# Down projection of a gated MLP in seven block products: all operand sums on VectorE, another order of the products, splits and sums on pairs of tiles

## The chip, the cores and the metric

The kernel runs on one core of a Trainium2 chip. The time is the device time of one launch in microseconds (us), the median of several executions. The core's engines work side by side, each through its own queue in order: PE (TensorE, matrix products into PSUM), DVE (VectorE, elementwise), ACT (ScalarE, elementwise with a function), POOL (GpSimd, elementwise here) and SP (SyncE, which in this kernel only issues DMA transfers). They are tied together by semaphores that a planner has placed.

## The reference, cut to what matters

One layer: three token mixers on 1024 tokens and 256 context tokens, merged into a residual stream, then a gated MLP with a depthwise convolution of three taps, then a final RMS norm. What the change touches is the last matrix product of the MLP and what follows it:

```python
def conv_ffn(h, w_up, w_dw, b_dw, w_down):
    a, g = jnp.split(dwconv(h @ w_up, w_dw, b_dw), 2, axis=-1)
    return (a * jax.nn.silu(g)) @ w_down          # (1024, 2816) @ (2816, 1024)
...
    x = x_mix + m_lat[:, :, 5] * conv_ffn(h, ...)
return rms_norm(x, norm_final)
```

All in fp32. The kernel computes an fp32 product by splitting each operand into a rounded high part and the rest (`hi`, `lo`), and adding three passes on PE: hi·hi, hi·lo, lo·hi.

## The kernel before

**The down projection** (from line 961 on, the last stage) is a 2 x 2 block product in Winograd's form, with seven block products instead of eight. The 2816 features are cut into two halves of 11 tiles of 128 (`KD = 11`), the 1024 tokens into two halves of 512 (`LH`), the 1024 output channels into two halves of four tiles. The activations lie in DRAM (`act_d`), as blocks B11 (first feature half, first token half), B12 (first, second), B21, B22; the weights as W11, W12, W21, W22 (`w_dn`). Each product `q` (0 to 6) multiplies one activation block or sum of blocks by one weight block or sum of blocks: 11 feature tiles x 4 output tiles x 3 passes = 132 matmuls of 128 x 128 by 512 columns. In `q` = 6 the loops are turned round (output tile outside), and its last output tile is done in 384 and 128 columns (`LAST`).

| q | activation operand | weight operand | PSUM set | added to `xt` afterwards (token half, first channel tile) |
|---|---|---|---|---|
| 0 | B11 | W11 | 0, new | (0, 0) |
| 1 | t = B22 - B12, on POOL | s = W11 - W21, on POOL | 1, new | (1, 4) |
| 2 | t + B11, on DVE | s = W22 - s, on POOL | 0, goes on | (1, 4), (0, 4), (1, 0) |
| 3 | B21 - t, on POOL | W22 | 1, goes on | (0, 4) |
| 4 | B12 - B11, on POOL | W11 + s, on POOL | 0, new | (1, 4) |
| 5 | B21 | W12; s = W12 - s on POOL for q = 6 | 1, new | (0, 0) |
| 6 | B22 | s | 0, goes on | (1, 0) |

`act(q, k)` (line 990) makes the activation operand of one feature tile: it loads what it needs (`load_b1`, and `stream`, which uses two buffers for B12 and three for the others), forms the sum, and calls `split`: a cast on ACT to `hi` (line 738) and a subtraction on DVE to `lo` (line 739), into one of 12 buffers `ac`. `weights(q, k0, nk)` (line 1032) does the same for the weights of two feature tiles (a pair; the eleventh is alone): raw weights through three buffers `wr`, a resident copy `dw` of 11 tiles that holds the running sum, and `w_split` (lines 1026 and 1027) into three buffers each of `wh` and `wl`. `dn` (lines 1067 to 1069) issues the three passes. After each product `add` (line 1075) adds the PSUM tiles, scaled by a channel's factor, to the residual `xt`, 36 additions in all (one of them in two pieces), in groups of four by `after` (line 1082). When a tile of `xt` is complete, `done` squares it on ACT and sums the squares, on POOL for the first of them (line 735). `final` scales by the norm and stores; two of its eight tiles go over POOL (line 1096).

**What sets the order.** A planner orders each engine's queue by priority, in the order of the program, with work moved ahead by `tc.high_priority(offset=...)`: sums and loads of a later unit come ahead of the earlier unit's matmuls by `APRIO + SPRIO` or `WPRIO + SPRIO` places. At run time each queue is strictly in order; an instruction that waits holds up all behind it, on SP too.

```python
  1004                        G.tensor_tensor(out=src, in0=b, in1=a, op=ALU.subtract)
  1051                        G.tensor_tensor(out=s, in0=s, in1=r, op=ALU.subtract)
  1055                        G.tensor_tensor(out=s, in0=r, in1=s, op=ALU.subtract)
  1082        after = (((0, 0, 0),), ((1, 4, 0),), ((1, 4, 0), (0, 4, 0), (1, 0, 0)), ((0, 4, 1),), ((1, 4, 1),), ((0, 0, 1),))
  1108            new = q in (0, 1, 4, 5)
```

(`G` is POOL, `V` is DVE, `A` is ACT, `T` is PE.)

Of the kernel before, what the change touches and what calls it, by code (L numbers as in the profile page):

```python
# [85 lines left out]
def build(tc, ins, out):  # L86
    nc = tc.nc
    V, A, G, T, SP = nc.vector, nc.scalar, nc.gpsimd, nc.tensor, nc.sync
    with ExitStack() as top:
# [635 lines left out]
        def sumsq(pool, parts, src, i, name, n, NPOOL):  # L725

            first = i in (0, NPOOL, KT - 1)
            sq = pool.tile([P, n], F32, tag="ss" if first and i < KT - 1 else "sq", name=f"ss{name}{i}",
                           bufs=3 if first and i < KT - 1 else 2)
            A.activation(sq, src, AF.Square)  # L730
            if first:
                parts.append(sq)
            else:
                e, q = (G, parts[0]) if i < NPOOL else (V, parts[1])
                e.tensor_tensor(out=q, in0=q, in1=sq, op=ALU.add)
# [228 lines left out]
        NRING = 12  # L964
        B11, B12, B21, B22 = range(4)
        b1 = [(pa if k < 8 else p2).tile([P, LH], F32, tag=f"b1_{k}", name=f"b1_{k}") for k in range(KD)]
        tt = {}
        dw = p2.tile([P, KD, 512], F32, tag="dw", name="dw")

        def load_b1(k):  # L970
            SP.dma_start(b1[k], act_d[k][:, t1])

        def stream(b, k, q):
            if b == B12:
                t = pc.tile([P, LH], F32, tag="sn", name=f"b{b}_{q}_{k}", bufs=2)
            else:
                t = p2.tile([P, LH], F32, tag="st", name=f"b{b}_{q}_{k}", bufs=3)
            SP.dma_start(t, act_d[b // 2 * KD + k][:, t2 if b % 2 else t1])
            return t

        def t_tile(k):
            if k not in tt:
                if k == KD - 1:
                    tt[k] = p2.tile([P, LH], F32, tag="tt", name="tt")
                else:
                    t = pc.tile([P, 2, LH], F32, tag="c", name=f"tt{k}", bufs=NC)
                    tt[k], tt[k + 1] = t[:, 0], t[:, 1]
            return tt[k]

        def act(q, k):  # L990
            j = (q * KD + k) % NRING
            t = pa.tile([P, 2, LH], F32R, tag=f"ac{j}", name=f"ac{q}_{k}")
            h = t[:, 0], t[:, 1]
            with tc.high_priority(offset=APRIO):
                with tc.high_priority(offset=SPRIO):
                    if q == 0:
                        load_b1(k)
                        src = b1[k]
                    elif q == 1:
                        if k < 2:  # L1000
                            load_b1(k)
                        a, b = stream(B12, k, q), stream(B22, k, q)
                        src = t_tile(k)
                        G.tensor_tensor(out=src, in0=b, in1=a, op=ALU.subtract)
                    elif q == 2:
                        src = tt[k]
                        V.tensor_tensor(out=src, in0=src, in1=b1[k], op=ALU.add)
                    elif q == 3:
                        b = stream(B21, k, q)
                        src = tt[k]  # L1010
                        G.tensor_tensor(out=src, in0=b, in1=src, op=ALU.subtract)
                    elif q == 4:
                        b = stream(B12, k, q)
                        src = b1[k]
                        G.tensor_tensor(out=src, in0=b, in1=src, op=ALU.subtract)
                    else:
                        src = stream((B21, B22)[q - 5], k, q)
                split(h, src)
            return h

        def w_split(src, nk, ncol):

            cnt[0] += 1
            hi, lo = (wp.tile([P, 1024], F32R, tag=t, name=f"{t}{cnt[0]}", bufs=n)[:, :nk * ncol]
                      .rearrange("p (k n) -> p k n", k=nk) for t, n in (("wh", WH), ("wl", WL)))
            A.copy(hi, src)
            V.tensor_tensor(out=lo, in0=src, in1=hi.bitcast(F32), op=ALU.subtract)  # L1027
            return hi, lo

        W11, W12, W21, W22 = (ins["w_dn"][j] for j in range(4))  # L1030

        def weights(q, k0, nk):

            def raw(src):
                cnt[0] += 1
                t = wp.tile([P, 1024], F32, tag="wr", name=f"wr{cnt[0]}", bufs=WR)[:, :nk * 512]
                t = t.rearrange("p (k n) -> p k n", k=nk)
                SP.dma_start(t, src[k0:k0 + nk].rearrange("f p t -> p f t"))
                return t

            s = dw[:, k0:k0 + nk]
            with tc.high_priority(offset=wprio[0]):
                with tc.high_priority(offset=SPRIO if q else 0):
                    if q == 0 and k0 >= 4:
                        SP.dma_start(s, W11[k0:k0 + nk].rearrange("f p t -> p f t"))
                        src = s
                    elif q == 1:
                        if k0 < 4:
                            SP.dma_start(s, W11[k0:k0 + nk].rearrange("f p t -> p f t"))
                        r = raw(W21)  # L1050
                        G.tensor_tensor(out=s, in0=s, in1=r, op=ALU.subtract)
                        src = s
                    elif q == 2:
                        r = raw(W22)
                        G.tensor_tensor(out=s, in0=r, in1=s, op=ALU.subtract)
                        src = s
                    else:
                        src = raw((W11, None, None, W22, W11, W12)[q])
                        if q == 4:
                            G.tensor_tensor(out=src, in0=src, in1=s, op=ALU.add)  # L1060
# [18 lines left out]
        def done(tb, i, n):  # L1079
            sumsq(p2, sss[tb], xts[tb][:, i], n, f"f{tb}", LH, NPOOL)  # L1080

        after = (((0, 0, 0),), ((1, 4, 0),), ((1, 4, 0), (0, 4, 0), (1, 0, 0)), ((0, 4, 1),), ((1, 4, 1),), ((0, 0, 1),))
# [18 lines left out]
        first = [(a0[0][:, f], a0[1][:, f]) for f in range(2)]  # L1101
        wprio[0] = WPRIO_D
        sets = [None, None]
        xload = [(tb, i) for tb, i0 in ((0, 0), (1, 4), (0, 4), (1, 0)) for i in range(i0, i0 + 4)]
        count = [0, 0]
        for q in range(6):
            st = q % 2
            new = q in (0, 1, 4, 5)
# [7 lines left out]
            for k0 in range(0, KD, 2):  # L1116
                nk = min(2, KD - k0)
                w = weights(q, k0, nk)
                for k in range(k0, k0 + nk):
                    h = first.pop(0) if first else act(q, k)  # L1120
                    for j in range(4):
                        dn(zs[j], [p[:, k - k0] for p in w], slice(j * P, (j + 1) * P), h, new and k == 0, k == KD - 1, **on)
                if pend and k0 == 2:
                    act_store()
                if k0 >= 4:
                    for _ in range(2 if q == 2 else 1):
                        if xload:
                            tb, i = xload.pop(0)
                            SP.dma_start(xts[tb][:, i], xm_d[tb, i])
                if q == 0 and k0 == 4:  # L1130
                    wprio[0] = WPRIO
            for tb, i0, end in after[q]:
                for j in range(4):
                    add(tb, i0 + j, zs[j])
                    if end:
                        done(tb, i0 + j, count[tb])
                        count[tb] += 1

        q = 6
        ss = sss[1]  # L1140
        xt = xts[1]
# [3 lines left out]
        for i in range(4):  # L1145
            ws = {}
            z0 = 0
            for n in LAST if i == 3 else (LH,):
                z = sets[0][i][:, z0:z0 + n]
                for f0 in range(0, KD, 8):  # L1150
# [4 lines left out]
                    for k in range(f0, f0 + nk):  # L1155
                        if k not in hs:
                            hs[k] = act(q, k)
                        dn(z, [p[:, k - f0] for p in ws[f0]], slice(0, P), [t[:, z0:z0 + n] for t in hs[k]],
                           False, k == KD - 1, skip_group_check=True)
                    if f0 == 0 and i == 0:  # L1160
                        norm = rms_r(p2, sss[0], LH, "f0", True)
                    if f0 == 0 and i == 1:
                        final("0", norm, xts[0], 0, LH)
# [4 lines left out]
                with tc.high_priority(offset=0 if prev is None else LPRIO):  # L1168
                    add(1, i, z, z0, n)
                    if i < 3:  # L1170
                        done(1, i, 4 + i)
                        continue
                    sq = p2.tile([P, n], F32, tag="sq", name=f"ssl{z0}", bufs=2)
                    A.activation(sq, xt[:, i, z0:z0 + n], AF.Square)
                    args = ([t[:, z0:z0 + n] for t in ss] + [sq], n, f"fl{z0}", True)
                    if prev is None:
                        prev = [args, xt, LH + z0, n]
# [3 lines left out]
        final("2", r, xt, L - n, n)  # L1181
# [545 lines left out]
```

## Time and profile before

| | us |
|---|---|
| median of 3 runs (lowest, highest) | 2101.91 (2099.66, 2103.96) |
| the profiled execution | 2102.28 |
| its span, first to last instruction | 2100.5 |

A profile shows one execution of the program. Times in its views are counted from the first instruction of the span. The page's first part gives each engine's busy time:

```profile
span 2100.5 us, 30318 instructions
## 1 busy us (share of the span) xinstructions
PE 2045.0 (97%) x11501; PEld 1706.9 (81%) x11501; DVE 1460.3 (70%) x2338; ACT 1009.6 (48%) x1776; POOL 413.1 (20%) x314
```

PEld is the loading of weights, which overlaps the matmuls. A matmul's recorded length contains its pipeline, so matmuls that follow one another start closer together than they are long. The second part cuts the span in 40 slices of 52.5 us, with the busy share in tenths:

```profile
PE   8999999999999999999999999999999999997997
DVE  4846656636665788577887747569778777769983
POOL 0000000010021232100000000011332343247752
PEclk9999999999999999999999999999999999998999
```

The down projection takes the last five slices, from 1846.4 us on.

### The profile page before, as it was taken

What the parts mean: (1) busy time and instruction counts of PE and PEld (TensorE: products, weight loads), DVE (VectorE), ACT (ScalarE), POOL (GpSimd) and SP (SyncE); (2) the same over time, 40 slices, a digit from 0 to 9 for tenths busy, and PEclk for the clock granted to TensorE, in tenths of its full rate; (3) what the DMA queues carried; (4) which work ended last, traced back from release to release, by engine and by line L of the source; (5) the groups of instructions that cost most, each with busy time, mean ns of one, the idle gap of its engine ahead of it and who ended that gap; (6) DMA issues with size and microseconds to landing.
All of it is one profiled execution on the core that took longest, in us unless ns stands there. A gap on an engine that the chain in (4) does not pass through costs nothing.

```text
span 2100.5 us, 30318 instructions
## 1 busy us (share of the span) xinstructions
PE 2045.0 (97%) x11501; PEld 1706.9 (81%) x11501; DVE 1460.3 (70%) x2338; ACT 1009.6 (48%) x1776; POOL 413.1 (20%) x314
## 2 busy tenths in 40 slices
PE   8999999999999999999999999999999999997997
PEld 5888888888988888878888788888888888885886
DVE  4846656636665788577887747569778777769983
ACT  3433333311122877688888734346444444443451
POOL 0000000010021232100000000011332343247752
PEclk9999999999999999999999999999999999998999
DMA  9411111136544311211110454541222222277442
GB/s 369 135 45 34 39 51 41 46 121 215 183 137 130 96 47 54 90 37 33 36 34 23 134 193 142 192 158 54 100 81 91 72 89 81 86 252 242 141 156 81
DMA packets 101746, 227.95 MB, mean 109 GB/s; under 512 B 10976, under 2 KB 35936, under 8 KB 100576
## 3 DMA queue, kind: packets, MB, share of 16 engines
q1 hardware_dynamic: 101600, 226.02, 32.6%
q8 instruction: 90, 1.47, 0.3%
q14 instruction: 56, 0.46, 0.1%
HBM read 180.37 MB, written 45.61 MB: 108 GB/s over the span
## 4 chain that ended last, share of the span: by engine, by line
PE 65%; DVE 4%; DMA 2%; issue 2%; ACT 2%; POOL 1%; SPq 0%; DVEq 0%; POOLq 0%; ACTq 0%
PE pp L1476 4%; PE gz L190 3%; PE gz L191 3%; PE gz L192 3%; PE dn L1069 3%; PE dn L1067 3%; PE dn L1068 3%; PE up L909 2%; PE up L910 2%; PE up L911 2%; PE po L1462 2%; PE po L1463 2%; PE br L191 2%; PE br L192 2%; PE br L190 2%
## 5 line engine op out<-in xcount | busy, mean ns | idle before, releaser
L166 ACT CAST wh<-wr 128x1024 fp32r<-128x1024 f32 x91 | 95.8, 1052 | 282.9 <-PE gz L191 50.8
L167 DVE TENSOR_TENSOR wl<-wr,wh 128x1024 fp32r<-128x1024 f32 x91 | 112.5, 1237 | 105.6 <-ACT wh L166 104.5
L1481 DVE TENSOR_TENSOR pl<-pp,ph 128x512 fp32r<-128x512 f32 x236 | 159.7, 688 | 29.4 <-ACT ph L1480 23.8
L190 PE MATMUL gz<-hh,wh 128*128 128x512 f32 x384 | 156.0, 407 | 3.2 <-ACT gs L580 3.1
L191 PE MATMUL gz<-hl,wh 128*128 128x512 f32 x384 | 152.4, 397 | 0.0
L192 PE MATMUL gz<-hh,wl 128*128 128x512 f32 x384 | 152.2, 397 | 0.0
L1480 ACT CAST ph<-pp 128x512 fp32r<-128x512 f32 x236 | 135.7, 585 | 31.5 <-PE pp L1476 28.8
L1069 PE MATMUL dn<-ac,wl 128*128 128x512 f32 (+2 forms) x311 | 121.5, 391 | 13.0 <-DVE wl L1027 12.8
L1068 PE MATMUL dn<-ac,wh 128*128 128x512 f32 (+2 forms) x311 | 121.0, 389 | 2.2 <-DVE ac L739 2.2
L1067 PE MATMUL dn<-ac,wh 128*128 128x512 f32 (+2 forms) x311 | 121.1, 390 | 1.4 <-DVE xt L1075 1.4
L201 PE MATMUL tm<-wl,hh 128*128 128x256 f32 x384 | 108.9, 283 | 2.4 <-DVE wl L167 2.4
L200 PE MATMUL tm<-wh,hh 128*128 128x256 f32 x384 | 108.7, 283 | 0.0
L202 PE MATMUL tm<-wh,hl 128*128 128x256 f32 x384 | 108.6, 283 | 0.0
L1462 PE MATMUL po<-ph,VHL 128*128 128x512 f32 x236 | 106.1, 449 | 1.6 <-ACT ph L1480 1.1
L1463 PE MATMUL po<-pl,VHL 128*128 128x512 f32 x236 | 97.4, 413 | 0.1
L190 PEld LDWEIGHTS gz<-hh,wh 128*128 128x128 f32 x384 | 72.7, 189 | 16.7 <-ACT gs L580 5.3
L192 PEld LDWEIGHTS gz<-hh,wl 128*128 128x128 f32 x384 | 72.6, 189 | 15.0
L191 PEld LDWEIGHTS gz<-hl,wh 128*128 128x128 f32 x384 | 72.8, 190 | 11.3
L1069 PEld LDWEIGHTS dn<-ac,wl 128*128 128x128 f32 x311 | 59.5, 191 | 26.5 <-DVE wl L1027 14.9
L1476 PE MATMUL pp<-ident,plat 128*128 128x128 f32 x512 | 76.6, 273 | 0.0
L201 PEld LDWEIGHTS tm<-wl,hh 128*128 128x128 f32 x384 | 73.7, 192 | 3.3 <-DVE wl L167 3.0
L1476 PEld LDWEIGHTS pp<-ident,plat 128*128 128x128 f32 x512 | 62.7, 140 | 16.8 <-DVE pl L1481 1.2
(1426 smaller groups left out, 6068.9 us busy)
## 6 DMA issues: line engine op xcount, KB each, us to landing
wr<-in_w_cm SPq DMA_DIRECT2D x48, 512.0 KB, 3.8
wr<-in_w_up SPq DMA_DIRECT2D x44, 512.0 KB, 3.5
b<-act_d SPq DMA_DIRECT2D x77, 256.0 KB, 3.5
wmr<-in_w_mod SPq DMA_DIRECT2D x32, 512.0 KB, 4.5
wr<-in_w_dn SPq DMA_DIRECT2D x27, 512.0 KB, 3.8
gate_d<-gs SPq DMA_DIRECT2D x48, 256.0 KB, 2.1
sgt<-gate_d SPq DMA_DIRECT2D x24, 512.0 KB, 3.3
act_d<-u SPq DMA_DIRECT2D x22, 512.0 KB, 2.6
```

The costliest lines, as they stand in the source:

```text
L190: T.matmul(psl, wh[:, k, c], hh[:, k0 + k, cols], start=s, stop=False)
L191: T.matmul(psl, wh[:, k, c], hl[:, k0 + k, cols], start=False, stop=False)
L192: T.matmul(psl, wl[:, k, c], hh[:, k0 + k, cols], start=False, stop=e)
L201: T.matmul(psl, hh[:, k, toks], wl[:, k % 4, :], start=False, stop=False)
L1067: T.matmul(z, w[0][:, c], h[0], start=s, stop=False, **on)
L1068: T.matmul(z, w[0][:, c], h[1], start=False, stop=False, **on)
L1069: T.matmul(z, w[1][:, c], h[0], start=False, stop=e, **on)
L1462: T.matmul(po, vv, ph, start=n == 0, stop=False)
L1463: T.matmul(po, vv, pl, start=False, stop=n == len(kts) - 1)
L1476: T.transpose(pp[:, h], PT(h, n), ident)
L1480: A.copy(ph, pp)
L1481: V.tensor_tensor(out=pl, in0=pp, in1=ph.bitcast(F32), op=ALU.subtract)
```

## The change

The seven products are formed from other sums and come in another order:

| q | activation operand | weight operand | PSUM set | added to `xt` afterwards |
|---|---|---|---|---|
| 0 | B11 | W11 | 0, new | (0, 0) |
| 1 | x = B12 - B11 | s = W22 + W21 | 1, new | (1, 4) |
| 2 | x = B22 - x | s = s - W11 | 0, goes on | (1, 0) |
| 3 | B22 | W12 - s | 1, goes on | (1, 0) |
| 4 | B11 - x | s = W22 - s | 0, goes on | (1, 4) |
| 5 | B21; x = B21 - x for q = 6 | W12; W22 is loaded into `dw` for q = 6 | 1, new | (0, 0) |
| 6 | x | W22 | 0, goes on | (0, 4) |

All sums are on DVE (`less`, and one addition), as are the sums of squares in `done`. A PSUM set is added to `xt` after each product and nowhere twice: 28 additions. Loads, sums and splits of the activations work on pairs of feature tiles (`u` from 0 to 5, the last one single), with six buffers `ac` of twice the size, and the streamed blocks take the five buffers `c` (pairs, too) that the up projection used, in place of the two and three single ones. In `q` = 0 the weights all go through `wr`.

```diff
-        def sumsq(pool, parts, src, i, name, n, NPOOL):
+        def sumsq(pool, parts, src, i, name, n, NPOOL, eng=G):
...
-                e, q = (G, parts[0]) if i < NPOOL else (V, parts[1])
+                e, q = (eng, parts[0]) if i < NPOOL else (V, parts[1])
...
-        NRING = 12
+        NRING = 6
+        UN = (KD + 1) // 2
...
+        nks = [min(2, KD - 2 * u) for u in range(UN)]
+        tx = [(pa if u < 4 else p2).tile([P, nks[u], LH], F32, tag=f"tx{u}", name=f"tx{u}") for u in range(UN)]
...
+        def stream(b, q, u):
+            return fetch(pc.tile([P, 2, LH], F32, tag="c", name=f"b{b}_{q}_{u}", bufs=NC)[:, :nks[u]], b, u)
+
+        def less(out, a, b):
+            V.tensor_tensor(out=out, in0=a, in1=b, op=ALU.subtract)
+
+        def act(q, u):
+            t = pa.tile([P, 2, 2, LH], F32R, tag=f"ac{(q * UN + u) % NRING}", name=f"ac{q}_{u}")
+            h = t[:, 0, :nks[u]], t[:, 1, :nks[u]]
+            x = tx[u]
             with tc.high_priority(offset=APRIO):
+                src = x
                 with tc.high_priority(offset=SPRIO):
...
+                    if q == 0 or q == 1 and u == 0:
+                        fetch(x, B11, u)
+                    if q == 1:
+                        less(x, stream(B12, q, u), x)
                     elif q == 2:
...
+                        less(x, stream(B22, q, u), x)
                     elif q == 3:
...
+                        src = stream(B22, q, u)
                     elif q == 4:
...
+                        src = stream(B11, q, u)
+                        less(src, x, src)
+                    elif q == 5:
+                        src = stream(B21, q, u)
+                        less(x, src, x)
                 split(h, src)
             return h
...
             s = dw[:, k0:k0 + nk]
             with tc.high_priority(offset=wprio[0]):
                 with tc.high_priority(offset=SPRIO if q else 0):
...
+                    src = s
+                    if q == 0:
+                        src = raw(W11)
                     elif q == 1:
...
+                        load(s, W21)
+                        V.tensor_tensor(out=s, in0=raw(W22), in1=s, op=ALU.add)
                     elif q == 2:
...
+                        less(s, s, raw(W11))
+                    elif q == 3:
+                        src = raw(W12)
+                        less(src, src, s)
+                    elif q == 4:
+                        less(s, raw(W22), s)
                     else:
...
+                        src = raw(W12)
                 w = w_split(src, nk, 512)
                 if q == 5:
-                    G.tensor_tensor(out=s, in0=src, in1=s, op=ALU.subtract)
+                    load(s, W22)
...
-        after = (((0, 0, 0),), ((1, 4, 0),), ((1, 4, 0), (0, 4, 0), (1, 0, 0)), ((0, 4, 1),), ((1, 4, 1),), ((0, 0, 1),))
+            sumsq(p2, sss[tb], xts[tb][:, i], n, f"f{tb}", LH, NPOOL, V)
+
+        after = ((0, 0, 0), (1, 4, 0), (1, 0, 0), (1, 0, 1), (1, 4, 1), (0, 0, 1))
...
-            new = q in (0, 1, 4, 5)
+            new = q in (0, 1, 5)
...
+            for u in range(UN):
+                w = weights(q, u)
+                h = act(q, u) if q or u else a0
...
-                        final("0", norm, xts[0], 0, LH)
+                        final("0", norm, xts[1], LH, LH)
...
-                    add(1, i, z, z0, n)
+                    add(0, 4 + i, z, z0, n)
```

More of the change, by code (lines that the diff above doesn't have):

```diff
@@ L962, in build @@
         p2 = Aligned(top.enter_context(tc.tile_pool(name="p2", bufs=1, reuse_waits="tile")))
-        NRING = 12
+        NRING = 6
+        UN = (KD + 1) // 2
         B11, B12, B21, B22 = range(4)
-        b1 = [(pa if k < 8 else p2).tile([P, LH], F32, tag=f"b1_{k}", name=f"b1_{k}") for k in range(KD)]
-        tt = {}
+        W11, W12, W21, W22 = (ins["w_dn"][j] for j in range(4))
+        nks = [min(2, KD - 2 * u) for u in range(UN)]
+        tx = [(pa if u < 4 else p2).tile([P, nks[u], LH], F32, tag=f"tx{u}", name=f"tx{u}") for u in range(UN)]
@@ L968, in build @@
         dw = p2.tile([P, KD, 512], F32, tag="dw", name="dw")
[L970 to L978, printed above, removed]
-            return t
[L981 to L993, printed above, removed]
+        def fetch(t, b, u):
+            f = b // 2 * KD + 2 * u
+            SP.dma_start(t, act_d[f:f + nks[u], :, t2 if b % 2 else t1].rearrange("f p t -> p f t"))
+            return t
+        def stream(b, q, u):
+            return fetch(pc.tile([P, 2, LH], F32, tag="c", name=f"b{b}_{q}_{u}", bufs=NC)[:, :nks[u]], b, u)
@@ L994, in act @@
+        def less(out, a, b):
[4 more added lines that the diff above has]
+            x = tx[u]
             with tc.high_priority(offset=APRIO):
+                src = x
                 with tc.high_priority(offset=SPRIO):
[L996 to L1004, printed above, removed]
+                    if q == 0 or q == 1 and u == 0:
+                        fetch(x, B11, u)
+                    if q == 1:
+                        less(x, stream(B12, q, u), x)
@@ L1005, in act @@
                     elif q == 2:
-                        src = tt[k]
-                        V.tensor_tensor(out=src, in0=src, in1=b1[k], op=ALU.add)
+                        less(x, stream(B22, q, u), x)
                     elif q == 3:
-                        b = stream(B21, k, q)
-                        src = tt[k]
-                        G.tensor_tensor(out=src, in0=b, in1=src, op=ALU.subtract)
+                        src = stream(B22, q, u)
                     elif q == 4:
-                        b = stream(B12, k, q)
@@ L1014, in act @@
[L1014 to L1017, printed above, removed]
+                        src = stream(B11, q, u)
[3 more added lines that the diff above has]
+                        less(x, src, x)
                 split(h, src)
@@ L1025, in w_split, with weights, load @@
                       .rearrange("p (k n) -> p k n", k=nk) for t, n in (("wh", WH), ("wl", WL)))
-            A.copy(hi, src)
-            V.tensor_tensor(out=lo, in0=src, in1=hi.bitcast(F32), op=ALU.subtract)
+            split((hi, lo), src)
             return hi, lo
-        W11, W12, W21, W22 = (ins["w_dn"][j] for j in range(4))
-        def weights(q, k0, nk):
+        def weights(q, u):
+            k0, nk = 2 * u, nks[u]
+            def load(t, src):
+                SP.dma_start(t, src[k0:k0 + nk].rearrange("f p t -> p f t"))
+                return t
             def raw(src):
@@ L1036, in raw @@
                 t = wp.tile([P, 1024], F32, tag="wr", name=f"wr{cnt[0]}", bufs=WR)[:, :nk * 512]
-                t = t.rearrange("p (k n) -> p k n", k=nk)
-                SP.dma_start(t, src[k0:k0 + nk].rearrange("f p t -> p f t"))
-                return t
+                return load(t.rearrange("p (k n) -> p k n", k=nk), src)
             s = dw[:, k0:k0 + nk]
@@ L1043, in weights @@
                 with tc.high_priority(offset=SPRIO if q else 0):
-                    if q == 0 and k0 >= 4:
-                        SP.dma_start(s, W11[k0:k0 + nk].rearrange("f p t -> p f t"))
-                        src = s
+                    src = s
+                    if q == 0:
+                        src = raw(W11)
                     elif q == 1:
[L1048 to L1052, printed above, removed]
-                    elif q == 2:
-                        r = raw(W22)
-                        G.tensor_tensor(out=s, in0=r, in1=s, op=ALU.subtract)
-                        src = s
-                    else:
-                        src = raw((W11, None, None, W22, W11, W12)[q])
-                        if q == 4:
-                            G.tensor_tensor(out=src, in0=src, in1=s, op=ALU.add)
+                        load(s, W21)
+                        V.tensor_tensor(out=s, in0=raw(W22), in1=s, op=ALU.add)
+                    elif q == 2:
+                        less(s, s, raw(W11))
[4 more added lines that the diff above has]
+                        less(s, raw(W22), s)
+                    else:
+                        src = raw(W12)
                 w = w_split(src, nk, 512)
                 if q == 5:
-                    G.tensor_tensor(out=s, in0=src, in1=s, op=ALU.subtract)
+                    load(s, W22)
             return w
@@ L1100, in build @@
         a0 = w_unit(act_d[0:2, :, :LH].rearrange("f p t -> p f t"), 2, LH)
-        first = [(a0[0][:, f], a0[1][:, f]) for f in range(2)]
         wprio[0] = WPRIO_D
+        xload = [(tb, i) for tb, i0 in ((0, 0), (1, 4), (1, 0), (0, 4)) for i in range(i0, i0 + 4)]
+        count = [0, 0]
         sets = [None, None]
-        xload = [(tb, i) for tb, i0 in ((0, 0), (1, 4), (0, 4), (1, 0)) for i in range(i0, i0 + 4)]
-        count = [0, 0]
         for q in range(6):
             st = q % 2
-            new = q in (0, 1, 4, 5)
+            new = q in (0, 1, 5)
             if new and st:
@@ L1115, in build @@
             on = dict(skip_group_check=not new)
[L1116 to L1120, printed above, removed]
+            for u in range(UN):
+                w = weights(q, u)
+                h = act(q, u) if q or u else a0
+                for k in range(nks[u]):
                     for j in range(4):
-                        dn(zs[j], [p[:, k - k0] for p in w], slice(j * P, (j + 1) * P), h, new and k == 0, k == KD - 1, **on)
-                if pend and k0 == 2:
+                        dn(zs[j], [p[:, k] for p in w], slice(j * P, (j + 1) * P), [t[:, k] for t in h],
+                           new and k == u == 0, 2 * u + k == KD - 1, **on)
+                if pend and u == 1:
                     act_store()
[L1125 to L1130, printed above, removed]
-                    wprio[0] = WPRIO
[L1132 to L1137, printed above, removed]
+                if u >= 2 and q < 4:
+                    tb, i = xload.pop(0)
+                    SP.dma_start(xts[tb][:, i], xm_d[tb, i])
+                if q == 0 and u == 2:
+                    wprio[0] = WPRIO
+            tb, i0, end = after[q]
+            for j in range(4):
+                add(tb, i0 + j, zs[j])
+                if end:
+                    done(tb, i0 + j, count[tb])
+                    count[tb] += 1
         q = 6
-        ss = sss[1]
-        xt = xts[1]
+        ss = sss[0]
+        xt = xts[0]
         hs = {}
@@ L1156, in build @@
                         if k not in hs:
-                            hs[k] = act(q, k)
+                            h = act(q, k // 2)
+                            for c in range(nks[k // 2]):
+                                hs[k + c] = [t[:, c] for t in h]
                         dn(z, [p[:, k - f0] for p in ws[f0]], slice(0, P), [t[:, z0:z0 + n] for t in hs[k]],
@@ L1160, in build @@
                     if f0 == 0 and i == 0:
-                        norm = rms_r(p2, sss[0], LH, "f0", True)
+                        norm = rms_r(p2, sss[1], LH, "f0", True)
                     if f0 == 0 and i == 1:
-                        final("0", norm, xts[0], 0, LH)
+                        final("0", norm, xts[1], LH, LH)
                     if prev is not None and f0 == 0:
@@ L1168, in build @@
                 with tc.high_priority(offset=0 if prev is None else LPRIO):
-                    add(1, i, z, z0, n)
+                    add(0, 4 + i, z, z0, n)
                     if i < 3:
-                        done(1, i, 4 + i)
+                        done(0, 4 + i, 4 + i)
                         continue
                     sq = p2.tile([P, n], F32, tag="sq", name=f"ssl{z0}", bufs=2)
-                    A.activation(sq, xt[:, i, z0:z0 + n], AF.Square)
+                    A.activation(sq, xt[:, 4 + i, z0:z0 + n], AF.Square)
                     args = ([t[:, z0:z0 + n] for t in ss] + [sq], n, f"fl{z0}", True)
                     if prev is None:
-                        prev = [args, xt, LH + z0, n]
+                        prev = [args, xt, z0, n]
                     else:
@@ L1180, in build @@
                 z0 += n
-        final("2", r, xt, L - n, n)
+        final("2", r, xt, LH - n, n)
 def forget(nc, pool, z, F, K, bounds, n, nm, tag=None):
```

1 line of the change is left out of this document (removed).

## The prediction, made before the changed kernel ran

> **What bounds the kernel now.** The first view is the span with its clock, the second the busy time of each engine in stretches. The stretches run from one product's first matmul to the next one's, then to the end of the last product and of the span; columns are length, busy time of PE, PEld, DVE, ACT and POOL with counts, the granted clock, the DMA share and GB/s.
>
> ```profile
> core 0: 2100.5 us, clock 0.993
> ```
> ```profile
> 1846.40:1877.20 30.80, 30.65 (x133) 24.55 (x132) 19.91 (x24) 13.22 (x19) 15.13 (x7) 1.00 0.75 274
> 1877.20:1926.30 49.10, 35.58 (x133) 27.62 (x132) 47.10 (x36) 17.57 (x27) 36.34 (x19) 0.83 0.73 246
> 1926.30:1958.10 31.80, 30.23 (x133) 24.68 (x133) 31.80 (x24) 12.12 (x17) 27.37 (x16) 1.00 0.63 207
> 1958.10:1988.00 29.90, 29.90 (x134) 24.76 (x133) 26.54 (x31) 11.91 (x17) 19.66 (x9) 1.00 0.50 158
> 1988.00:2018.00 30.00, 30.00 (x134) 24.84 (x133) 25.87 (x22) 15.09 (x23) 20.54 (x9) 1.00 0.50 159
> 2018.00:2047.90 29.90, 29.90 (x133) 24.78 (x132) 25.14 (x26) 16.31 (x27) 13.99 (x8) 1.00 0.42 132
> 2047.90:2087.50 39.60, 38.16 (x212) 33.13 (x210) 15.34 (x23) 8.98 (x14) 10.40 (x7) 1.00 0.15 54
> 2087.50:2100.50 13.00, 1.69 (x10) 1.21 (x10) 5.51 (x15) 1.05 (x3) 4.19 (x6) 0.68 0.48 162
> ```
>
> Products 3, 4 and 5 take 29.9 us each with PE never idle: 132 matmuls at 0.227 us. That is PE's floor. Products 0, 1 and 2 take 30.8 + 49.1 + 31.8 = 111.7 us, against 3 x 29.9 = 89.7. **22.0 us** are lost there, 19.2 of them in product 1, where DVE is busy for 47.1 of 49.1 us. The third view, the chain of work that ended last, shows how; the fourth (timeline) gives POOL and the two longest stalls of PE.
>
> ```profile
> 1903.62 2.80 DVE tt L1007
> 1906.42 5.54 DVE ac L739 x2
> 1911.97 2.74 DVE tt L1007
> 1914.71 1.15 DVE wl L1027
> ...
> 1916.70 0.43 PE dn L1067
> ...
> 1920.96 0.43 PE dn L1068
> 1921.39 0.32 PE dn L1069
> 1921.70 0.23 PE dn L1067
> ```
> ```profile
> 1903.42 10.74 POOL L1055 TENSOR_TENSOR dw<-wr,dw 128x1024 f32<-128x1024 f32 x4 [0.95 <-DMA wr<-in_w_dn]
> 1900.79 0.80 PE L1069 MATMUL dn<-ac,wl 128*128 128x512 f32 x1 [5.07 <-DVE wl L1027]
> 1915.90 0.79 PE L1069 MATMUL dn<-ac,wl 128*128 128x512 f32 x1 [6.14 <-DVE wl L1027]
> ```
>
> While POOL forms four weight sums for product 2 (10.74 / 4 = 2.7 us each), DVE's small operations for product 1 take 2.7 to 2.8 us each, one to each POOL operation, and PE waits for `wl`. What they take without POOL is seen around 1857, where POOL has yet to start (its first sum is at 1859.0, in the `L1051` row below) and the DMA engines are full (timeline, then the stretch; the third row is from later):
>
> ```profile
> 1854.67 3.10 DVE L739 TENSOR_TENSOR ac<-b,ac 128x512 fp32r<-128x512 f32 x5
> 1857.69 2.36 DVE L1027 TENSOR_TENSOR wl<-dw,wh 128x1024 fp32r<-128x1024 f32 x2
> 2047.51 2.07 DVE L1075 SCALAR_TENSOR_TENSOR xt<-dn,mods,xt 128x512 f32<-128x512 f32 x3
> ```
> ```profile
> 1846.40:1857.00 10.60, 10.59 (x47) 8.46 (x46) 10.38 (x13) 6.95 (x11) 0.00 (x0) 1.00 1.00 366
> ```
>
> 3.10 / 5 = 0.62 us for 512 columns, 2.36 / 2 = 1.18 for 1024, 2.07 / 3 = 0.69 for an addition from PSUM. The view of one line (shortest, median, longest ns) tells who is stretched:
>
> ```profile
> L1007 DVE TENSOR_TENSOR tt<-tt,b x11: 679/694/2879, 1869.5 to 1922.8; 128x512 f32<-128x512 f32 x11
> L1075 DVE SCALAR_TENSOR_TENSOR xt<-dn,mods,xt x37: 351/739/751, 1884.1 to 2087.5; 128x512 f32<-128x512 f32 x35, 128x384 f32<-128x384 f32 x1, 128x128 f32<-128x128 f32 x1
> L1051 POOL TENSOR_TENSOR dw<-dw,wr x6: 1713/2406/5049, 1859.0 to 1897.9; 128x1024 f32<-128x1024 f32 x5, 128x512 f32<-128x512 f32 x1
> L735 POOL TENSOR_TENSOR ssf<-ssf,ssf x10: 1281/1730/2285, 1993.7 to 2068.5; 128x512 f32<-128x512 f32 x10
> ```
>
> Operations that read two SBUF tensors go up to four times their price, those that read one from PSUM never (751 ns at most), and POOL's stretch as well. So product 1 is bound by DVE and POOL getting in each other's way.
>
> **The change, part by part.** *PE* keeps its matmuls: seven products of 132, product 6 in the same pieces.
>
> *POOL's sums go to DVE.* I count product by product, with a "set" for one operation over the 11 feature tiles: five pairs and a single, 5 x 1.18 + 0.62 = 6.5 us. Products 1 and 2: activation sum, weight sum and two splits, four sets, plus four additions at 0.69: 26.0 + 2.8 = 28.8 us each. Product 3: three sets and four additions, 22.3. Product 4: four sets, four additions and three sums of squares at 0.62, 30.7. Product 5: three sets, four additions, two sums of squares, 23.5. Together 134.1 us in the 149.5 that PE needs for the five. Measured now are 47.1 + 31.8 + 26.5 + 25.9 + 25.1 = 156.4, so DVE takes over POOL's work and is still busy for 22 us less. Product 4 is 0.8 us over its 29.9; product 3, with 7.6 to spare, covers it if work runs ahead. It can: three buffers of split weights and six of split activations are three units and one whole product (a unit, a pair of tiles, is 24 matmuls, 5.4 us). If that cover were gone, product 4 would cost those 0.8.
>
> *The stall of products 0 to 2 goes:* -22.0 us, if nothing else is late. What is next is PE itself, then DVE at 28.8 of 29.9. Part of the 22.0 is clock: after the 6.14 us stall eleven matmuls start 0.43 apart instead of 0.23, 2.2 us. The Trainium skill, "TensorE: Matmul & The Clock Gate", section "What's actually happening", says that an idle window of about 3.4 us halves the clock until PE has been busy for another. By that, leftover stalls shorter than this cost their own length only, and longer ones more; the row above agrees for a stall of 6.14.
>
> *Pairs.* The first unit of product 0 that `act` makes now needs a cast and a subtraction of 1024 columns before the first matmuls, in place of 512:
>
> ```profile
> L738 ACT CAST ac<-b 128x512 fp32r<-128x512 f32 x42 | 25.0, 617 | 23.9 <-DMA b<-act_d 18.3 <-PE dn L1069 5.6
> L1026 ACT CAST wh<-dw 128x1024 fp32r<-128x1024 f32 x17 | 17.7, 1049 | 14.8 <-PE dn L1068 9.3 <-DMA dw<-in_w_dn 2.1 <-DVE wl L1027 1.8
> ```
>
> 1.05 - 0.62 + 1.18 - 0.62 = 1.0 us, once, since no lead exists there yet: +1.0 (bounds 0, as the loads may be first, and 3). Elsewhere pairs lie under PE. ACT, at most 17.6 us a product now, keeps its work.
>
> *Eight additions fewer* lie on DVE in product 2's place and are in the count. The sums of squares of product 6 (five of the ten in `L735` are of this token half) aren't what its end waits for: the row of PE's waits for DVE there is the additions, which stay, as does the tail of 13.0 us.
>
> ```profile
> PE dn L1067 <- DVE xt L1075: 1.4, 3, 0.7
> ```
>
> *Loads.* The tiles of 256 KB, by count of the code: 66 of activations for the 77 below, 88 of weights for 70. SP's queue is in order, and what held it before were POOL and DVE.
>
> ```profile
> b<-act_d SPq DMA_DIRECT2D x77, 256.0 KB, 3.5
> wr<-in_w_dn SPq DMA_DIRECT2D x27, 512.0 KB, 3.8
> ```
> ```profile
> SPq L1038 <- DVE wl L1027: 31.9, 7, 7.0
> SPq L978 <- POOL tt L1004: 25.3, 7, 8.5
> ```
>
> The second wait goes; the streams now have five pair buffers that wait for DVE. What is added is DVE's own wait: a `less` whose load is late holds the splits behind it in DVE's queue, and PE waits for those. I cost loads at nothing: DVE, PE and the lead of three units (16 us) hide landings of 4 us. If the cover goes, see the second rival.
>
> *Small DVE waits.* DVE now has slack of 1.1 us in each of products 1 and 2. In product 1 it stood waiting for ACT as follows:
>
> ```profile
> DVE ac L739 <- ACT ac L738: 6.0, 2, 4.2
> ```
>
> In product 0 DVE is idle 30.8 - 19.9 = 10.9 us, in which it can get ahead. How much of such waiting reaches PE no row shows. Bounds: 0 and 13; I take 2, near the lower end, because the lead of product 0 stands against it.
>
> Sum: 2102.28 - 22.0 + 1.0 + 2.0 = 2083.3 for the profiled execution. That execution is 0.4 above the median of the three runs, so the same number serves: **2083 us**. Its own range is 2079 (nothing lost, and a microsecond gained at the end) to 2088.
>
> **The rivals.**
> 1. *DVE becomes the bound by waiting in order.* With 6.0 us of waits in each of products 1, 2 and 4, they need 34.8, 34.8 and 36.7 us, 16.6 over the floor; about 5 is covered by the lead from product 0. 2080.3 + 1.0 + 11.6 = 2093. For it: 96% use of DVE. Against: the rings are deep, and the price of 1.18 is from the longer end (an operation starts 2.36 - 1.22 = 1.14 after the one before).
> 2. *Loads become the bound in product 1.* It needs 11 + 11 weight tiles, 13 activation tiles and 4 of `xt`: 39 x 0.262 MB = 10.2 MB. At the 274 GB/s of the first stretch this takes 37.3 us, 7.4 over: 2089. Against: the row at 366 GB/s, by which it takes 27.9, and loads issued in product 0. The Trainium skill, "DMA: Bandwidth & Descriptors", section "Where 436 GB/s comes from", puts HBM to one core at about 358 GB/s; by that it is 28.5 us and hidden.
> 3. *The lead is lost, and it is slower.* If SP or DVE holds a wait so early that a unit's loads start only when the unit before is done, each unit costs its chain: landing 3.8, sum 1.18, cast 1.05, split 1.18, 7.2 us against 5.4. That is 1.8 x 6 = 10.8 a product, 43 in products 1 to 4: 2124. It decides from the third product on, where it exceeds 22. For it: 32 and 25 us of waits of SP. Against: three `wr` and five stream buffers would all have to be useless.
> 4. *The stretch isn't POOL's doing.* Then DVE keeps its mean of 1.7 for 1024 columns and 1.45 for 512, and product 1 needs 20 x 1.7 + 4 x 1.45 + 2.8 = 42.6 us, 13 over, as do products 2 and 4: 2080 + 39 = 2119. Against: the unstretched rows at full DMA, and `L1075`.
>
> ```profile
> L739 DVE TENSOR_TENSOR ac<-tt,ac 128x512 fp32r<-128x512 f32 x17 | 24.3, 1450 | 6.0 <-ACT ac L738 6.0
> L1027 DVE TENSOR_TENSOR wl<-dw,wh 128x1024 fp32r<-128x1024 f32 (+1 forms) x6 | 10.4, 1734 | 0.0
> ```
>
> **How the numbers follow.** Forecast 0.62; rival 1, 0.14; rival 2, 0.10; a sum of both that gives the gain back to within 0.2% (4 us, about what a measurement of this kernel can tell from no change), 0.05; rival 3, 0.06; rival 4, 0.03. Faster: 0.62 + 0.14 + 0.10 = 0.86; same 0.05; slower 0.09. The range goes from 2079 over both faster rivals to 2097, leaving out 0.14 and a little of their edges.
>
> **What would show it.** In the changed profile product 1 should take 30 to 32 us, DVE about 29 of them at a clock of 1.00, POOL almost nothing before the norms, and no two-input operation of 512 columns over 0.75 us. If DVE's waits stand for ACT or DMA in product 1 and PE's for `wl` or `ac`, rival 1 or 2 holds; if DMA stays below 0.9 there, not the second. Wrong would be: a stretched DVE without POOL, or a product 3 to 5 above 31 us, which the prediction takes to be PE's alone.

## The result, and the profile after

| | before | after |
|---|---|---|
| median, us (lowest, highest) | 2100.94 (2099.66, 2103.96), 4 runs | 2081.89 (2081.25, 2083.23), 4 runs |
| the profiled execution, us | 2102.28 | 2082.49 |
| its span, us | 2100.5 | 2080.7 |

The ratio is 0.9908, with a 95% interval from 0.9891 to 0.9925: 0.9% faster, with an interval of under 0.2% to each side. Forecast were 2083 us, in a range from 2079 to 2097.

The busy times in stretches, cut at the first matmul of each product as before (length, PE, PEld, DVE, ACT, POOL, clock, DMA share, GB/s; products 0 to 6, then the tail):

```profile
1847.20:1878.00 30.80, 30.26 (x133) 24.71 (x133) 27.62 (x26) 15.19 (x16) 0.00 (x0) 1.00 1.01 373
1878.00:1907.90 29.90, 29.90 (x133) 24.78 (x132) 29.54 (x30) 12.63 (x13) 0.00 (x0) 1.00 0.87 311
1907.90:1937.80 29.90, 29.90 (x133) 24.77 (x132) 26.73 (x28) 12.12 (x13) 0.00 (x0) 1.00 0.80 273
1937.80:1967.70 29.90, 29.90 (x133) 24.76 (x133) 29.37 (x31) 11.17 (x12) 0.00 (x0) 1.00 0.67 231
1967.70:1997.60 29.90, 29.90 (x134) 24.76 (x133) 23.38 (x26) 13.58 (x16) 0.00 (x0) 1.00 0.63 200
1997.60:2027.60 30.00, 30.00 (x134) 24.83 (x133) 17.55 (x20) 14.81 (x19) 0.00 (x0) 1.00 0.09 27
2027.60:2067.20 39.60, 38.16 (x212) 33.15 (x210) 20.52 (x31) 11.16 (x18) 4.48 (x3) 1.00 0.15 53
2067.20:2080.70 13.50, 1.69 (x10) 1.20 (x10) 5.49 (x15) 1.46 (x4) 4.19 (x6) 0.65 0.46 156
```

Products 1 and 2 now take PE's floor of 29.9 us, as 3 to 5 did already. Products 0 to 2 together went from 111.7 to 90.6 us, 21.1 less. The span is 19.8 shorter, since the down projection began 0.8 us later (1847.2 for 1846.4) and its tail took 13.5 us for 13.0. The later beginning isn't the change's doing as far as these runs show: no line of the stages before was changed in what it does, and in the runs below the beginning lies anywhere from 1842.4 to 1847.4. The longer tail is: from the last addition to the end of the span it takes 13.0 to 13.1 us in the kernel before and its three variants below, and 13.4 to 13.5 in the changed kernel and its five. What lengthens it stays open.

DVE in product 1 (timeline: start, length, how often), where its operations took 2.7 us and more:

```profile
1888.56 1.22 DVE L739 TENSOR_TENSOR wl<-dw,wh 128x1024 fp32r<-128x1024 f32 x1
1889.70 0.69 DVE L981 TENSOR_TENSOR tx<-b,tx 128x512 f32<-128x512 f32 x1
1890.30 0.68 DVE L1036 TENSOR_TENSOR dw<-wr,dw 128x512 f32<-128x512 f32 x1
```

Every one has its unstretched length, and the next starts 1.14 or 0.60 us later. The one stretched two-input operation of the stage, a sum of squares of 1.78 us at 2039.97 in product 6, lies beside the two operations that `final` leaves on POOL, from 2039.46 on. All that PE still waits for in this stage (the waits, with total, times and longest; the first row belongs to the final norm):

```profile
PE rpf L260 <- POOL rsfl L250: 3.0, 2, 2.0
PE dn L1052 <- DVE xt L1060: 1.2, 2, 0.7
PE dn L1053 <- DVE ac L739: 0.5, 1, 0.5
```

### The profile page after: what moved, and what is told of

It is laid out like the page before. It is cut to its first block, busy times and chain, and to the rows that moved or that the text cites. A ratio compares the mean times of both kernels' runs of the same rounds, so it can differ in the third digit from the quotient of the medians.

```text
span 2080.7 us, 30085 instructions
## 1 busy us (share of the span) xinstructions
PE 2038.4 (98%) x11501; PEld 1704.3 (82%) x11501; DVE 1443.1 (69%) x2343; ACT 1005.1 (48%) x1742; POOL 274.1 (13%) x247
## 3 DMA queue, kind: packets, MB, share of 16 engines
q1 hardware_dynamic: 102000, 227.85, 32.9%
## 4 chain that ended last, share of the span: by engine, by line
PE 68%; DVE 3%; ACT 2%; issue 1%; DMA 1%; POOL 1%; SPq 0%; DVEq 0%; ACTq 0%; POOLq 0%
PE pp L1460 5%; PE dn L1053 3%; PE dn L1054 3%; PE dn L1052 3%; PE gz L190 3%; PE gz L191 3%; PE gz L192 3%; PE up L909 3%; PE up L911 2%; PE up L910 2%; PE po L1446 2%; PE po L1447 2%; PE br L191 2%; PE br L192 2%; PE br L190 2%; PE upc L911 2%
## 5 line engine op out<-in xcount | busy, mean ns | idle before, releaser
L190 PE MATMUL br<-yh,wh 128*128 128x512 f32 x192 | 74.3, 390 | 1.4 <-ACT yh L1605 1.4
```

What stands on the lines that cost most here:

```text
L190: T.matmul(psl, wh[:, k, c], hh[:, k0 + k, cols], start=s, stop=False)
```

## The experiments

Two theories were set against each other. **A**: POOL and DVE held each other up in reading SBUF, and putting the sums on DVE is what counts. **B**: the other order of the products, the pairs of tiles, the deeper stream buffers and the eight additions fewer did it. A kernel's stretches are cut at its own products. The kernel before was run again beside each group: 2097.51 us in the first group and 2100.47 in the second. Ratios are to it.

### The change without its engine

The changed kernel, sums back on POOL:

```diff
         def less(out, a, b):
-            V.tensor_tensor(out=out, in0=a, in1=b, op=ALU.subtract)
+            G.tensor_tensor(out=out, in0=a, in1=b, op=ALU.subtract)
...
-                        V.tensor_tensor(out=s, in0=raw(W22), in1=s, op=ALU.add)
+                        G.tensor_tensor(out=s, in0=raw(W22), in1=s, op=ALU.add)
...
-            sumsq(p2, sss[tb], xts[tb][:, i], n, f"f{tb}", LH, NPOOL, V)
+            sumsq(p2, sss[tb], xts[tb][:, i], n, f"f{tb}", LH, NPOOL, G)
```

> The changed kernel with one thing put back: every operand sum and every sum of squares of the down projection on POOL instead of DVE; order of the products, pairs, rings and the 28 additions stay. Theory A (the stall came from POOL and DVE holding each other up, and the engine of the sums is what counts): products 1 and 2 need 12 pair sums each on POOL at 2.4 us or more, 29 us each, and DVE's splits are stretched again to 2 us and more, so the stall is back: 2095 to 2125 us, product 1 at 40 us or longer. Theory B (the gain came from the other order, the pairs and the deeper stream buffers): 2080 to 2086 us, products 1 to 5 at 29.9.

Measured: 2109.52 us, ratio 1.0052 (1.0035 to 1.0069). Its products 1 to 4, in stretches:

```profile
1873.20:1905.20 32.00, 30.45 (x133) 24.60 (x132) 30.86 (x15) 9.91 (x11) 32.00 (x12) 1.00 0.81 285
1905.20:1948.20 43.00, 34.73 (x133) 27.35 (x133) 37.09 (x21) 15.13 (x16) 37.40 (x13) 0.88 0.60 202
1948.20:1978.10 29.90, 29.90 (x133) 24.78 (x132) 29.90 (x16) 9.16 (x10) 25.62 (x10) 1.00 0.51 176
1978.10:2022.90 44.80, 33.11 (x134) 26.36 (x134) 31.82 (x19) 15.21 (x19) 33.15 (x14) 0.85 0.56 195
```

The stall is back, and larger than before: 2.1 + 13.1 + 14.9 = 30.1 us. Theory B falls. The place was missed: product 1 gets by with 32.0 us, since six of the sums were formed in product 0 already (18.6 us of POOL), and products 2 and 4 pay. In the 37.1 us that DVE is busy in product 2, its 21 operations take 1.8 us on average, with POOL busy beside it for 37.4.

Product 4 is another matter. PE's longest stall there comes from a wait for one of POOL's results (timeline, ACT, then PE):

```profile
2003.71 0.63 ACT L730 ACTIVATE ssf<-xt 128x512 f32<-128x512 f32 x1 [17.61 <-POOL ssf L735]
2005.33 0.79 PE L1052 MATMUL dn<-ac,wh 128*128 128x512 f32 x1 [10.71 <-ACT wh L738]
```

ACT stood 17.6 us before a square until POOL had worked off the sums of squares (`ssf`), which stood behind operand sums in its queue, and the weight cast that PE needed stood behind that square. So this run mixes stretched DVE operations with waits in POOL's queue. POOL also has more to do than in the kernel before, where product 2's activation sum is on DVE: it is busy for 162.4 us in products 0 to 6, against 143.4.

### The engine without the rest of the change

The kernel before, with all `G.tensor_tensor` of lines 1004 to 1063 made `V.tensor_tensor`, and the sums of squares of `done` on DVE.

```diff
-                        G.tensor_tensor(out=src, in0=b, in1=a, op=ALU.subtract)
+                        V.tensor_tensor(out=src, in0=b, in1=a, op=ALU.subtract)
...
-                        G.tensor_tensor(out=s, in0=s, in1=r, op=ALU.subtract)
+                        V.tensor_tensor(out=s, in0=s, in1=r, op=ALU.subtract)
...
```

> The kernel before with one thing done: its operand sums and sums of squares of the down projection on DVE instead of POOL; its order of products, single tiles, stream buffers of two and three, and its 36 additions stay. Theory A: most of the 22 us go, 2081 to 2087 us, products 1 to 5 within 32 us each. Theory B: the streams still wait for two and three single buffers, product 1 stays at 40 us or longer, 2095 to 2105 us. In between (2087 to 2095) both have a share.

Measured: 2080.49 us, ratio 0.9910 (0.9889 to 0.9931), the changed kernel's ratio within 0.0002. Products 1 to 4:

```profile
1878.40:1908.40 30.00, 30.00 (x134) 24.82 (x134) 29.53 (x40) 14.00 (x21) 0.00 (x0) 1.00 0.92 319
1908.40:1938.30 29.90, 29.90 (x134) 24.77 (x133) 29.71 (x44) 14.11 (x20) 0.00 (x0) 1.00 0.68 230
1938.30:1968.20 29.90, 29.90 (x133) 24.77 (x132) 28.33 (x40) 11.24 (x16) 0.00 (x0) 1.00 0.52 175
1968.20:1998.10 29.90, 29.90 (x133) 24.78 (x132) 26.27 (x33) 15.96 (x25) 0.00 (x0) 1.00 0.54 176
```

The whole gain is there with the old order, single tiles, two and three stream buffers and 36 additions. What the rest of the change gives is room on DVE: in products 1 to 5 DVE is busy 136.3 us here (with 22.45 in product 5) and 126.6 in the changed kernel. None of it shows in the time, as far as these intervals can tell.

### POOL beside DVE, with nothing depending on it

The changed kernel with 24 added POOL operations on a tile of their own:

```diff
+        junk = p2.tile([P, 1024], F32, tag="junk", name="junk")
+        G.memset(junk, 1.0)
         for q in range(6):
...
+                if q < 4:
+                    G.tensor_tensor(out=junk, in0=junk, in1=junk, op=ALU.mult)
```

> The changed kernel with 24 added POOL operations that nothing waits for: each multiplies a tile of 128 x 1024 of its own by itself, one after the other, from the start of the down projection on. They carry no dependence to any other work, so only a shared resource can make them felt. Theory A: while they run (24 x 2.4 us or more, some 60 to 90 us), DVE's operations with two SBUF inputs take 2 to 3.6 us, the additions from PSUM stay at 0.75, and PE stalls by 15 to 60 us: 2097 to 2140 us. Theory B (what held DVE and PE were waits on POOL's results): no change, 2080 to 2086 us.

Measured: 2110.42 us in one run. The timeline, POOL first, then DVE while it lasts and behind it:

```profile
1842.87 65.99 POOL L1106 TENSOR_TENSOR junk<-junk 128x1024 f32<-128x1024 f32 x24
```
```profile
1892.87 2.91 DVE L1036 TENSOR_TENSOR dw<-wr,dw 128x1024 f32<-128x1024 f32 x1
1895.70 2.91 DVE L739 TENSOR_TENSOR wl<-dw,wh 128x1024 fp32r<-128x1024 f32 x1
1898.54 2.91 DVE L739 TENSOR_TENSOR ac<-tx,ac 128x1024 fp32r<-128x1024 f32 x1
...
1909.87 1.21 DVE L739 TENSOR_TENSOR ac<-tx,ac 128x1024 fp32r<-128x1024 f32 x1
```

The two engines take turns: one DVE operation to each POOL operation, one every 2.83 us (1898.54 - 1895.70 = 2.84). With 1.14 for DVE's own, POOL's turn is 1.7. The moment POOL's row ends, at 1842.87 + 65.99 = 1908.86, DVE is back at 1.21. PE pays for it: products 0 and 1, in stretches, take 46.8 and 44.5 us in place of 30.8 and 29.9.

```profile
1844.50:1891.30 46.80, 35.73 (x133) 27.36 (x131) 46.77 (x19) 12.16 (x13) 45.47 (x18) 0.85 0.51 188
1891.30:1935.80 44.50, 34.86 (x133) 27.82 (x133) 44.50 (x34) 14.70 (x15) 17.09 (x7) 0.85 0.70 246
```

No result of the added operations is awaited, so this stall is not a wait on POOL's results. In the kernel before, such waits can't have cost product 1 much either, since DVE was idle for only 2.0 of its 49.1 us.

What was expected of the additions from PSUM this run can't tell: the first four run at 1914.41, when POOL has ended. The kernel before shows it, in product 1 (timeline, POOL, then DVE):

```profile
1897.93 1.71 POOL L1051 TENSOR_TENSOR dw<-dw,wr 128x512 f32<-128x512 f32 x1
1898.44 0.74 DVE L1075 SCALAR_TENSOR_TENSOR xt<-dn,mods,xt 128x512 f32<-128x512 f32 x1
1899.10 1.63 DVE L1027 TENSOR_TENSOR wl<-dw,wh 128x1024 fp32r<-128x1024 f32 x1
```

The addition, which reads one SBUF tensor, keeps its 0.74 us under a POOL operation; the split behind it, which reads two, is stretched.

The second kernel replaces the multiplication by two memsets, which write the same tile and read nothing:

```diff
-                    G.tensor_tensor(out=junk, in0=junk, in1=junk, op=ALU.mult)
+                    for _ in range(2):
+                        G.memset(junk, 1.0)
```

> As the run with the 24 POOL multiplications, but with 48 POOL memsets of 128 x 1024, which write SBUF and read nothing. If DVE and POOL collide in reading SBUF only, DVE's operations stay at 1.22 us for 1024 columns and the time at 2080 to 2086 us. If any activity of POOL on SBUF stretches DVE, its operations go to 2 us and more while the memsets run, and the time to 2090 us or more.

Measured: 2080.08 us in one run. POOL and DVE from 1847 to 1940 us, about products 0 to 2, by line (count, busy us, mean ns):

```profile
L1107 POOL MEMSET junk<- 128x1024 f32 x45 | 43.0, 956 | 2.6
L739 DVE TENSOR_TENSOR ac<-tx,ac 128x1024 fp32r<-128x1024 f32 x14 | 16.9, 1217 | 1.1 <-ACT ac L738 1.1
```

43 us of POOL writing beside them leave DVE's operations at 1.22 us. So the collision is in reading SBUF: POOL's reads against DVE's operations with two SBUF inputs. The Trainium skill, "SBUF — State Buffer", section "Who interferes with whom", says that such a DVE instruction contends with a GpSimd instruction that reads SBUF and not with one that only writes, and that the ports the two share are an exclusive lock. Both rows, 2.91 against 1.22, agree.

### How much room DVE has

The changed kernel with each weight sum formed twice, the first time into a tile that nothing reads:

```diff
+            def twice(r, s, nk):
+                less(junk[:, :nk * 512].rearrange("p (k n) -> p k n", k=nk), r, s)
...
                     elif q == 2:
-                        less(s, s, raw(W11))
+                        r = raw(W11)
+                        twice(r, s, nk)
+                        less(s, s, r)
```

(and the same in products 1, 3 and 4)

> The changed kernel with each weight sum of products 1 to 4 formed twice on DVE, the first time into a tile that nothing reads: 24 operations more, 4 x 6.3 = 25 us of DVE. In the changed kernel DVE is busy for 136.6 of the 150.4 us of products 0 to 4, so 14 us are free. Theory A (DVE is next to bound): the free time is used up and some 11 us reach PE, 2088 to 2098 us, DVE busy for over 29 us in each of products 1 to 4. If DVE had more room than its busy time shows, or the lead didn't hold, the time would be 2080 to 2085, or 2105 and more (25 us on the path).

Measured: 2088.99 us, ratio 0.9940 (0.9920 to 0.9961). Products 1 to 4:

```profile
1876.60:1906.60 30.00, 30.00 (x134) 24.82 (x134) 30.00 (x31) 10.72 (x11) 0.00 (x0) 1.00 0.79 272
1906.60:1938.50 31.90, 30.43 (x133) 24.58 (x132) 31.90 (x33) 14.53 (x15) 0.00 (x0) 1.00 0.65 226
1938.50:1968.40 29.90, 29.90 (x133) 24.77 (x132) 29.90 (x31) 8.63 (x9) 0.00 (x0) 1.00 0.66 219
1968.40:2004.10 35.70, 31.97 (x133) 25.78 (x133) 35.70 (x38) 16.94 (x19) 0.00 (x0) 0.95 0.71 237
```

DVE is busy without a break for four products, and of 25 us of added work 2.0 + 5.8 = 7.8 reach PE, where 11 were expected. The stage took up the other 17: in products 0 to 4 DVE had 13.8 us free (150.4 less 136.6) and now has 1.2 (in product 0, 30.7 less 29.46), and 3.7 us of its work moved on into product 5 (21.27 against 17.55). DVE is the next bound, and most of it is paid in the last of the four products.

### Half of the sums on DVE

The kernel before with only `weights`' sums on DVE, and with only `act`'s. The edits are those of the second experiment, for lines 1051 to 1063 in the one and 1004 to 1015 in the other; the sums of squares stay on POOL.

> The kernel before with only the weight sums on DVE; activation sums (1.3 us each without contention) and sums of squares stay on POOL. If the long weight sums, 2.4 to 2.8 us each and in a row, were what held DVE in product 1: 2080 to 2087 us. If any two-input work on POOL is enough: 11 activation sums on POOL hold up DVE by up to 1.3 us each, 14 us a product, product 1 at 33 us or longer and 2088 us or more.

> The kernel before with only the activation sums on DVE; weight sums and sums of squares stay on POOL. If the long weight sums were what held DVE: 2092 us or more, with product 1 at 38 us or longer, since they still come in a row beside product 1's splits. If the total of POOL's work counts, half of the 22 us go: 2086 to 2092. If it was only POOL's own queue being too full: 2080 to 2086.

Measured: 2095.18 us, ratio 0.9978 (0.9965 to 0.9990), with the weight sums on DVE; 2099.03, ratio 0.9989 (0.9979 to 0.9999), with the activation sums. Products 1 to 3 of the first, then products 1 and 2 of the second:

```profile
1875.90:1906.60 30.70, 30.14 (x134) 24.63 (x132) 30.70 (x34) 12.84 (x19) 8.02 (x6) 1.00 0.77 257
1906.60:1939.50 32.90, 30.66 (x133) 24.69 (x134) 30.93 (x31) 14.31 (x21) 21.59 (x11) 1.00 0.67 229
1939.50:1975.60 36.10, 33.16 (x134) 26.44 (x133) 28.07 (x31) 12.11 (x18) 16.55 (x11) 0.91 0.46 154
```
```profile
1876.20:1918.90 42.70, 32.49 (x134) 25.55 (x132) 40.89 (x40) 14.81 (x23) 24.10 (x9) 0.88 0.77 270
1918.90:1954.30 35.40, 33.07 (x133) 26.79 (x134) 30.76 (x46) 14.60 (x22) 0.00 (x0) 0.90 0.58 203
```

The weight sums held most of product 1: without them on POOL it takes 30.7 us, with them 42.7, and 49.1 in the kernel before. The second run came as its first branch said (2092 us or more, product 1 at 38 or longer). The first run fits neither of its branches whole: product 1 came down, but the time did not come to 2080 to 2087 us, since products 2 to 5 now stall (32.9, 36.1, 32.1 and 32.7 us). In the longest of these, product 3, the chain of work that ended last shows what PE waited for:

```profile
1946.86 5.57 DVE xt L1075 x9
1952.43 4.18 DMA wr<-in_w_dn
1956.71 1.05 ACT wh L1026
1957.79 1.96 DVE wl L1027
```

A weight load starts only at 1952.43, as the ninth addition ends, and PE waits for the cast and the split that follow it. In SP's queue this load stood behind four loads of activations, and SP's largest wait in this product, 11.9 us in all, is for POOL's activation sums to free a stream buffer. So the longest wait of this product is for a late load; taking turns with POOL adds 0.8 us to it (the split's 1.96 for 1.14). The two halves gain 0.2% and 0.1%, the whole 0.9%. How the loss of the halves divides, over all products, between taking turns and waits in a queue stays open.

### A version with less left to wait for

Apart from the final norm, what PE waits for in the changed kernel is the additions between output tiles of product 6 and the first pair of product 0. The changed kernel, with the output tiles of product 6 in another order, and the first pair that `act` makes split tile by tile:

```diff
-        for i in range(4):
+        for p_, i in enumerate((0, 2, 1, 3)):
...
-                split(h, src)
+                if q == 0 and u == 1:
+                    for k in range(2):
+                        split([p[:, k] for p in h], src[:, k])
+                else:
+                    split(h, src)
```

(`p_` takes `i`'s place where the norm is started and where the sums of squares are counted.)

> The changed kernel with two small things against what PE still waits for: in product 6 the output tiles go in the order 0, 2, 1, 3, so that the matmuls of a tile don't follow the addition from the other bank of the same two-bank PSUM tile (two gaps of 1.0 and 1.1 us), and the first pair of activations in product 0 is split tile by tile (a gap of 0.7 us). If these gaps are what they look like: 2.0 to 2.8 us less than the changed kernel, 2079 to 2081 us by a ratio to the kernel before of 0.988 to 0.990. If the waits only move (to DVE's next addition, or to loads): within 0.5 us of the changed kernel.

Measured: 2077.88 us, ratio 0.9892 (0.9869 to 0.9914). Products 0 and 6:

```profile
1844.90:1875.10 30.20, 30.19 (x133) 24.70 (x132) 27.53 (x27) 15.18 (x17) 0.00 (x0) 1.00 1.00 368
2024.70:2062.40 37.70, 37.44 (x212) 33.13 (x210) 19.53 (x30) 11.34 (x18) 3.58 (x3) 1.00 0.15 56
```

30.8 - 30.2 and 39.6 - 37.7: 2.5 us less, as expected; the ratio is as expected too, the time itself 1.1 us below. The ratios' intervals overlap with the changed kernel's, so the times alone don't tell the two apart; the stretches do.

## Why the prediction was right, point by point

- **What bounds the kernel.** Products 0 to 2 lose 22.0 us because POOL's and DVE's operations hold each other up: right for the 21.1 of products 1 and 2; the 0.9 of product 0 stayed with POOL idle. The engine alone brings the gain (0.9910), the change without the engine loses it (1.0052), and POOL reads that nobody waits for make such a stall anew.
- **The stall goes, -22.0.** It measured -21.1: 19.2 in product 1, 1.9 in product 2, nothing in product 0.
- **Pairs, +1.0.** In product 0 nothing was lost against before (30.8 and 30.8): the stall of PE on the first pair (0.5 us waiting for `ac`, and the restart) takes the place of three smaller ones, in which PE's weight load waited for `ac`, `wh` and `wl` (0.4, 0.3 and 0.6 us). Split singly, product 0 takes 30.2, so the pair costs 0.6.
- **Small DVE waits, +2.0.** None reached PE in products 1 to 5. The choice near the lower bound was right and the rest of it too cautious.
- **DVE's budget.** 134.1 us were counted for products 1 to 5, 126.6 measured. The price of 1.18 was too high (1.14 from start to start), and DVE did part of the work in product 0, where it was busy for 27.6 us instead of 19.9. So the distribution was off by far (product 3 at 29.4 where 22.3 were counted), the sum by 6%.
- **Loads, nothing.** Right, by prefetch: the DMA engines were full for all of product 0 (1.01, 373 GB/s, above each of the three rates that rival 2 was weighed with), and 0.87 busy in product 1, where the rival's own count by 274 GB/s asked for 37.3 us. The rate it took was one that waits had set, not the loads.
- **The rivals.** DVE as the bound (2093) did not come, with DVE 99% busy in product 1 (29.54 of 29.90); it begins about 17 us of DVE work further on. The lost lead (2124) did not come: DVE's first sums for products 1 and 2 start at 1861.65 and 1893.17, 16.4 and 14.7 us before the first matmul of their product, about the three units that were counted. That the stretch isn't POOL's doing (2119) is refuted by the two runs with added POOL work.
- **The sum.** 2083 was forecast and 2082.49 profiled. The large term came as counted. That the rest comes out within a microsecond is luck: 3.0 us of new stalls that the total does not show are made up for by a stage that began 0.8 later in this execution, 0.9 of stall that stayed in product 0, and the tail, which was taken to stay and grew by 0.5.

## What to carry to other kernels

Where DVE operations show a median at their price and a maximum at that price plus a POOL operation, moving POOL's elementwise work to DVE can leave DVE less busy than it was: 165.6 us in products 0 to 5 with only the engine changed, against 176.4 before. Count DVE's budget by the unstretched prices, stage by stage, against the bound of that stage, and move all of POOL's two-input work there or expect little: in this kernel half of it gained 0.1 and 0.2% where the whole gained 0.9%. And an engine at 99% need not hold up the one behind it, as long as its buffers let it run ahead.

## What was not expected of the hardware

While POOL's reads came without a break, DVE's operations on two SBUF tensors and POOL's alternated, one each: 2.83 us a turn, for a DVE operation of 1.14. A POOL memset of 128 x 1024 (0.96 us) beside them costs DVE nothing. And without the engine, the changed order was worse than the kernel before by 0.5%, with the stall in products 2 and 4 instead of 1. Two reasons are on record, POOL's further set of sums and ACT's wait for POOL in product 4. A third is likely but not shown: pairs make each POOL operation longer (3.3 us on average for the `tx` sums), and DVE waits for a whole one each time. Single tiles in the new order were not tried on POOL.
